# Gathers that take their row numbers straight from the picks, without small index tiles from ScalarE

## The chip, the cores and the metric

The kernel runs on one core of a Trainium2 chip. The metric is the device time of one execution in microseconds. The engines are named as a profile names them: PE (TensorE), DVE (VectorE), ACT (ScalarE), POOL (GpSimd, which here issues the indirect loads) and SP (SyncE, which here issues nearly all other loads and stores). PEld is the loading of weights into PE, which runs beside the matmuls.

## The reference, cut to what matters

One layer of an encoder: two gated token mixers, then a retrieval over 128 x 128 single-neuron experts (PEER). Only the last part is touched by the change. For each of 512 tokens and 8 heads, 16 experts are picked by a product of two sets of 128 keys; each picked expert has a row in `u_tab` and a row in `v_tab`, both 16384 x 1024 in float32.

```
q = (t @ w_q).reshape(n_tok, PEER_HEADS, 2, PEER_HALF)
sc = jnp.einsum("thpk,hpnk->thpn", q, sub_keys)
s_top, i_top = lax.top_k(sc, PEER_TOPK)
...
idx = jnp.take_along_axis(cand_idx..., pos, axis=-1)      # 8 heads x 16 picks for each token
g = jax.nn.softmax(best, axis=-1)
ue = u_tab[ib]
act = jax.nn.gelu(jnp.einsum("phkd,pd->phk", ue, tb))
ve = v_tab[ib]
out = jnp.einsum("phk,phkd->pd", gb * act, ve)
```

## The kernel before

The 512 tokens are four tiles of 128. Tiles 1 to 3 (384 tokens) are done **densely**: every one of the 16384 experts is multiplied with every token, and a gate matrix that is zero outside the picks selects. Tile 0 is done by **gathers**: for each of its 128 picks per token (8 heads x 16), an indirect load brings 128 rows of `u_tab` (one for each token of the tile, 512 KB) and later 128 rows of `v_tab` into a row buffer in SBUF, and DVE consumes it. That is 256 gathers, `ru0` to `ru127` and `rv0` to `rv127`.

The program has four parts in time: the mixers (to about 400 us), the keys and picks (to about 580), the gate matrix (to about 798), and the **last stage**, a loop over 128 **key pairs** `i` (one block of 128 rows of `v_tab`). For each `i` of the last stage:

- SP loads `raw_v` (512 KB, seven `raw` buffers shared with `raw_u`), `gt` (the gates, 128 KB, four buffers) and, for the late `i`, `hr` (192 KB); ACT and DVE split `raw_v` into `hi_v` and `lo_v` (three buffers, shared with the split of `raw_u`).
- DVE makes `wf` from gates and activations (L849, L850), ACT rounds it to `wh` (L851), DVE takes the rest `wl` (L852).
- PE does 18 matmuls of 512 columns into six accumulators (`v_mm`, L831, L832, L835).
- For the first 66 of the 128 pairs there is also one block of `u` to be turned into activations (`h_tile`, L392): `raw_u`, `hi_u`, `lo_u`, then 24 matmuls of 384 columns (L147 to L149), then a gelu into `hg`.
- Gathers are stepped: `gather_steps(pace[i], GLEFT)` records `pace[i]` gathers and, for each, the DVE instruction (L373 for `ru`, L387 for `rv`, SCALAR_TENSOR_TENSOR, called **the consumption** below) of the gather that lies four back (`drain(left)` with `GLEFT` = 4).

Eight gathers are made in the gate stage. The other 248 are spread over the pairs by weight, 2 for a pair with an `h_tile` and `GTAIL` = 0.5 after that:

```python
    wts = [2 if i < NKEY - nlag else GTAIL if i < NKEY - 4 else 0 for i in range(NKEY)]
    pace, done = [], 0
    for i in range(NKEY):
        want = -(-ng * sum(wts[:i + 1]) // sum(wts))
        pace.append(int(want) - done)
```

The row buffers of the last stage come from two pools in turn, three in `gp` (`GR`) and four in `dp` (`DR`), so an even gather reuses the buffer of the gather six before it, an odd one that of the gather eight before it. Gathers run in the order of `gsched`: 32 of `u`, 16 of `v`, and then 16 of `u` and 16 of `v` in turn, to the last 16 of `v`.

Up to the last stage the order on each engine is written by hand (`pinned()`). In the last stage it is not: the build places the instructions on each engine by its own reckoning of when their inputs are there. Only instructions that are given to `tc.keep_in_program_order` keep their place among each other: the gathers on POOL, and before the change the index tiles on ACT.

An index tile `eix` is a copy of up to four columns of picks (`eall`, float32) to int32, made by ACT in key pair `i` for the gathers of that pair (`gather_release`, L658 to L670). `ei0` holds the same picks as int32 for all 128 columns; it is finished in the second part of the program.

Of the kernel before, what the change touches and what calls it, by code (L numbers as in the profile page):

```python
# [11 lines left out]
I32 = mybir.dt.int32  # L12
U32 = mybir.dt.uint32
AF = mybir.ActivationFunctionType
# [3 lines left out]
P = 128  # L18
# [42 lines left out]
def tile_block(ctx: ExitStack, tc: tile.TileContext, x, w_in, vecs, w_ax, w_out, n2row, w_q, skT,  # L61
               uT, u_tab, v_tab, frow, out):
    nc = tc.nc
    sync, act, dve, pool, pe = nc.sync, nc.scalar, nc.vector, nc.gpsimd, nc.tensor
# [33 lines left out]
    def load(src, name, nsub=None):  # L98
        raw = strm.tile([P, D], F32, tag="raw", name=f"raw_{name}", bufs=RB)
        dst = raw if nsub is None else raw.rearrange("p (a b) -> p a b", a=nsub)  # L100
        sync.dma_start(dst, src)
        return raw

    def split(raw, name, lo_eng, pl=None):
        hi = (pl or strm).tile([P, D], F32R, tag="hi", name=f"hi_{name}", bufs=SB)
        lo = (pl or strm).tile([P, D], F32R, tag="lo", name=f"lo_{name}", bufs=SB)
        act.activation(hi, raw, AF.Copy)  # L107
        lo_eng.tensor_tensor(lo, raw, hi, op=ALU.subtract)  # L108
        return hi, lo
# [237 lines left out]
    eall = gp.tile([P, NTT, P], F32, name="eall")  # L347
    gall = gp.tile([P, NTT, P], F32, name="gall")
    ei0 = gp.tile([P, P], I32, name="ei0")
# [2 lines left out]

    ha = ctx.enter_context(tc.tile_pool(name="ha", bufs=1))

    gidx = {}
    rpool = [(gp, GR)]
    gcnt = [0]

    def gather(tab, n, name):
        ix = gidx.get(name, ei0[:, n:n + 1])  # L360
        rp, nb = rpool[gcnt[0] % len(rpool)]
        gcnt[0] += 1
        rows = rp.tile([P, D], F32, tag="rows", name=name, bufs=nb)
        ins = pool.indirect_dma_start(out=rows, out_offset=None, in_=tab,  # L364
                                in_offset=bass.IndirectOffsetOnAxis(ap=ix, axis=0))
        tc.keep_in_program_order(ins)
        return rows
# [8 lines left out]
    def drain(left):  # L376
        while len(dq) > left:
            dq.pop(0)()
# [31 lines left out]
    def h_get(i):  # L410
        if i not in hg:
            hg[i] = ha.tile([P, TD], F32, tag="hg", name=f"hr{i}", bufs=AHEAD)
            sync.dma_start(hg[i], hd[i - (NKEY - SPILL)])
        return hg[i]
# [230 lines left out]
    gsched = []  # L645
# [9 lines left out]
        gsched.append((gather_v, n))  # L655
    gpos = [0]

    def gather_release(n, i):  # L658
        names, p = [], gpos[0]
        while len(names) < n and p < len(gsched):  # L660
            f, a = gsched[p]
            if f is not gather_w:
                names.append(("ru" if f is gather_u else "rv") + str(a))
            p += 1
        if names:
            t = dp.tile([P, 4], I32, tag="eix", name=f"eix{i}", bufs=4)
            for m, nm in enumerate(names):
                c = int(nm[2:])
                tc.keep_in_program_order(act.activation(t[:, m:m + 1], eall[:, 0, c:c + 1], AF.Copy))  # L669
                gidx[nm] = t[:, m:m + 1]  # L670

    def gather_steps(n, left=0):
        while n > 0 and gpos[0] < len(gsched):
            f, a = gsched[gpos[0]]
            f(a)
            drain(left)
            gpos[0] += 1
            if f is not gather_w:
                n -= 1
# [108 lines left out]
    dp = ctx.enter_context(tc.tile_pool(name="dp", bufs=1))  # L788
# [7 lines left out]
    pace, done = [], 0  # L796
# [43 lines left out]
    for i in range(NKEY):  # L840
        raw = vr.pop(i) if i in vr else load(v_tab[i * P:(i + 1) * P, :], f"v{i}")
        hi, lo = split(raw, f"v{i}", dve)
        gt = dp.tile([P, TG], F32, tag="gt", name=f"gt{i}", bufs=4)
        sync.dma_start(gt, gd[i])
        wf = dp.tile([P, TD], F32, tag="wf", name=f"wf{i}", bufs=2)
        wh = strm.tile([P, TD], F32R, tag="wh", name=f"wh{i}", bufs=3)
        wl = strm.tile([P, TD], F32R, tag="wl", name=f"wl{i}", bufs=3)
        hv_ = h_get(i)
        dve.tensor_tensor(wf[:, :TG], gt, hv_[:, :TG], op=ALU.mult)  # L849
        dve.tensor_tensor(wf[:, TG:], stg[:, i, :], hv_[:, TG:], op=ALU.mult)  # L850
        act.activation(wh, wf, AF.Copy)  # L851
        dve.tensor_tensor(wl, wf, wh, op=ALU.subtract)  # L852
        if i < NKEY - LATE:
            for t in range(NDT):
                v_mm(i, t, hi, lo, wh, wl)
        else:
            late.append((hi, lo, wh, wl))
        if hn < NKEY:
            h_tile(hord[hn], dve)
            hn += 1  # L860
        gather_release(pace[i], i)
        gather_steps(pace[i], GLEFT)
        if i == NKEY - LATE - 1:
            for j in range(i + 1, NKEY):
                vr[j] = load(v_tab[j * P:(j + 1) * P, :], f"v{j}")
            fgb = dp.tile([P, D], F32, tag="rows", name="fgb", bufs=DR)
            sync.dma_start(fgb, frow.partition_broadcast(P))
            x2s.extend(load(x2d[t], f"x2s{t}") for t in range(NTT))
            x2s.append(dp.tile([P, D], F32, tag="rows", name="junk", bufs=DR))
            drain(0)  # L870
            finish(0)
# [50 lines left out]
```

## Time and profile before

| | us |
|---|---|
| median of 3 runs | 1619.49 (1616.62 to 1621.41) |
| the profiled execution | 1619.77 |
| its span, first to last instruction | 1617.7 |
| PE busy | 1597.2 (99%) |
| DVE busy | 1265.1 (78%) |
| ACT busy | 688.3 (43%) |
| POOL busy | 517.1 (32%) |

The granted clock of PE was 0.999 of full over the span. Matmuls are pipelined, so that a matmul's own duration is about twice the distance to the next one; "busy" therefore hides short gaps, and the distance between key pairs on PE is the better measure.

### The profile page before, as it was taken

Reading aid. Unit: us, or ns where it says so; the run is one execution under the profiler, and the core shown is the slowest. Engines: PE = TensorE matmul, PEld = TensorE weight load, DVE = VectorE, ACT = ScalarE, POOL = GpSimd, SP = SyncE. Lnnn points to the kernel's source line nnn. Section 1 sums busy time; section 2 is a strip of 40 time slices with the busy share of each in tenths; the row PEclk is TensorE's granted clock in tenths of the full one; section 3 lists DMA queues with packets and bytes.
Section 4 is the critical chain, followed back from the end, with each engine's and each line's share of the span. In section 5 each row is a group of like instructions: output and inputs, shape, how many; then the busy total and the mean of one; then the engine's idle time right before and its main releaser. Section 6 shows DMA issues by size and latency. Waiting matters only on the chain.

```text
span 1617.7 us, 23570 instructions
## 1 busy us (share of the span) xinstructions
PE 1597.2 (99%) x8402; PEld 1411.7 (87%) x8402; DVE 1265.1 (78%) x2404; ACT 688.3 (43%) x1222; POOL 517.1 (32%) x379
## 2 busy tenths in 40 slices
PE   9999999999999999999999999999999999999998
PEld 8888888888988999999999889999988998788776
DVE  6666666635999998676878888888888888777776
ACT  7444444434333454444533433333343443333334
POOL 0000000003787840000044444546544554223321
PEclk9999999999999999999999999999999999999999
DMA  6222222334333356969499999999999999998884
GB/s 242 95 94 95 95 95 95 91 112 175 107 124 111 126 177 191 305 214 301 153 324 323 342 328 332 341 332 334 340 323 350 324 347 367 328 308 292 289 304 150
DMA packets 158453, 379.09 MB, mean 234 GB/s; under 512 B 14080, under 2 KB 78592, under 8 KB 158208
## 3 DMA queue, kind: packets, MB, share of 16 engines
q1 hardware_dynamic: 112832, 230.25, 41.5%
q0 software_dynamic: 36864, 134.23, 23.6%
q10 hardware_dynamic: 8640, 13.11, 2.3%
q8 instruction: 65, 1.06, 0.3%
q14 instruction: 52, 0.43, 0.1%
HBM read 345.56 MB, written 31.98 MB: 233 GB/s over the span
## 4 chain that ended last, share of the span: by engine, by line
PE 64%; DMA 12%; DVE 10%; issue 6%; POOL 3%; ACT 2%; SPq 2%; DVEq 0%; ACTq 0%; POOLq 0%
PE pin L149 6%; PE pin L148 6%; PE pin L147 6%; PE ph L147 6%; PE ph L149 6%; PE ph L148 6%; PE acc L832 6%; PE acc L835 5%; PE acc L831 5%; DMA rv<-in_v_tab_dram,eix 5%; DMA ru<-in_u_tab_dram,eix 4%; DMA gd<-stg 2%; PE pq L147 2%; PE pq L149 2%; PE pq L148 2%
## 5 line engine op out<-in xcount | busy, mean ns | idle before, releaser
L147 PE MATMUL ph<-a1h,hi_u 128*128 128x384 f32 x1024 | 346.2, 338 | 0.0
L149 PE MATMUL ph<-a1h,lo_u 128*128 128x384 f32 x1024 | 343.6, 336 | 0.4 <-POOL lo_u L108 0.4
L148 PE MATMUL ph<-a1l,hi_u 128*128 128x384 f32 x1024 | 342.7, 335 | 0.0
L832 PE MATMUL acc<-lo_v,wh 128*128 128x512 f32 x768 | 301.4, 392 | 5.9 <-DVE lo_v L108 5.7
L831 PE MATMUL acc<-hi_v,wh 128*128 128x512 f32 x768 | 299.5, 390 | 0.0
L364 POOL DMA_INDIRECT rv<-in_v_tab_dram,eix x128 | 171.8, 1342 | 258.0 <-ACT eix L669 211.1
L835 PE MATMUL acc<-hi_v,wl 128*128 128x512 f32 x768 | 238.8, 390 | 0.0
L364 POOL DMA_INDIRECT ru<-in_u_tab_dram,eix x120 | 163.8, 1365 | 218.6 <-ACT eix L669 186.1
L387 DVE SCALAR_TENSOR_TENSOR acc<-rv,w,acc 128x1024 f32<-128x1024 f32 x128 | 164.7, 1287 | 81.3 <-DMA rv<-in_v_tab_dram,eix 81.2
L107 ACT ACTIVATE hi_v<-raw_v 128x1024 fp32r<-128x1024 f32 x128 | 135.0, 1054 | 184.2 <-PE ph L148 166.6
L373 DVE SCALAR_TENSOR_TENSOR ru<-ru,t 128x1024 f32<-128x1024 f32 x128 | 155.5, 1222 | 52.7 <-DMA ru<-in_u_tab_dram,eix 50.1
L148 PEld LDWEIGHTS ph<-a1l,hi_u 128*128 128x128 f32 x1024 | 192.4, 188 | 2.6
L147 PEld LDWEIGHTS ph<-a1h,hi_u 128*128 128x128 f32 x1024 | 192.3, 188 | 2.6
L149 PEld LDWEIGHTS ph<-a1h,lo_u 128*128 128x128 f32 x1024 | 192.2, 188 | 1.2 <-POOL lo_u L108 0.8
L851 ACT ACTIVATE wh<-wf 128x384 fp32r<-128x384 f32 x128 | 67.1, 525 | 269.8 <-PE acc L832 181.0
L832 PEld LDWEIGHTS acc<-lo_v,wh 128*128 128x128 f32 x768 | 144.2, 188 | 40.7 <-DVE lo_v L108 12.1
L149 PE MATMUL pin<-a1h,lo_in 128*128 128x512 f32 x448 | 174.4, 389 | 0.3 <-POOL lo_in L108 0.3
L148 PE MATMUL pin<-a1l,hi_in 128*128 128x512 f32 x448 | 174.4, 389 | 0.0
L147 PE MATMUL pin<-a1h,hi_in 128*128 128x512 f32 x448 | 174.3, 389 | 0.0
L835 PEld LDWEIGHTS acc<-hi_v,wl 128*128 128x128 f32 x768 | 144.1, 188 | 30.7
L831 PEld LDWEIGHTS acc<-hi_v,wh 128*128 128x128 f32 x768 | 144.1, 188 | 27.3 <-ACT hi_v L107 0.2
L108 DVE TENSOR_TENSOR lo_v<-raw_v,hi_v 128x1024 fp32r<-128x1024 f32 x128 | 156.1, 1219 | 2.7 <-ACT hi_v L107 2.6
(199 smaller groups left out, 2470.2 us busy)
## 6 DMA issues: line engine op xcount, KB each, us to landing
raw_u<-in_uT_dram SPq DMA_DIRECT2D x128, 512.0 KB
raw_v<-in_v_tab_dram SPq DMA_DIRECT2D x128, 512.0 KB
raw_in<-in_w_in_dram SPq DMA_DIRECT2D x56, 512.0 KB
gd<-stg SPq DMA_DIRECT2D x8, 2048.0 KB
gt<-gd SPq DMA_DIRECT2D x128, 128.0 KB
hd<-hg ACTq DMA_DIRECT2D x56, 192.0 KB
hr<-hd SPq DMA_DIRECT2D x56, 192.0 KB
raw_q<-in_w_q_dram SPq DMA_DIRECT2D x16, 512.0 KB
```

The costliest lines, as they stand in the source:

```text
L107: act.activation(hi, raw, AF.Copy)
L108: lo_eng.tensor_tensor(lo, raw, hi, op=ALU.subtract)
L147: pe.matmul(pt, wh(k), xh(k), start=start and m == 0, stop=False)
L148: pe.matmul(pt, wh(k), xl(k), start=False, stop=False)
L149: pe.matmul(pt, wl(k), xh(k), start=False, stop=stop and m == n - 1)
L364: ins = pool.indirect_dma_start(out=rows, out_offset=None, in_=tab, in_offset=bass.IndirectOffsetOnAxis(ap=ix, axis=0))
L373: dq.append(lambda: dve.scalar_tensor_tensor(rows, rows, 1.0, t0, op0=ALU.mult, op1=ALU.mult, accum_out=d0[:, n:n + 1]))
L387: dq.append(lambda: dve.scalar_tensor_tensor(acc0, rows, w0[:, n:n + 1], acc0, op0=ALU.mult, op1=ALU.add))
L831: pe.matmul(accs[t][h], wh[:, ts], hi[:, hsl], start=first, stop=False)
L832: pe.matmul(accs[t][h], wh[:, ts], lo[:, hsl], start=False, stop=False)
L835: pe.matmul(accs[t][h], wl[:, ts], hi[:, hsl], start=False, stop=last)
L851: act.activation(wh, wf, AF.Copy)
```

## The change

The index tiles are gone, with the ACT instructions that made them; every gather takes its row numbers from `ei0`.

```diff
-    gidx = {}
     rpool = [(gp, GR)]
     gcnt = [0]
 
     def gather(tab, n, name):
-        ix = gidx.get(name, ei0[:, n:n + 1])
+        ix = ei0[:, n:n + 1]
...
-    def gather_release(n, i):
-        names, p = [], gpos[0]
-        while len(names) < n and p < len(gsched):
-            f, a = gsched[p]
-            if f is not gather_w:
-                names.append(("ru" if f is gather_u else "rv") + str(a))
-            p += 1
-        if names:
-            t = dp.tile([P, 4], I32, tag="eix", name=f"eix{i}", bufs=4)
-            for m, nm in enumerate(names):
-                c = int(nm[2:])
-                tc.keep_in_program_order(act.activation(t[:, m:m + 1], eall[:, 0, c:c + 1], AF.Copy))
-                gidx[nm] = t[:, m:m + 1]
...
-        gather_release(pace[i], i)
         gather_steps(pace[i], GLEFT)
```

PE's order is the same before and after. On the other engines the build places instructions differently. In the rows below the number after a tile's first name is its key pair or gather; `lo_v36` is the split of pair 36, `ru64` the 65th gather of `u`.

DVE in the middle of the last stage, before: the seven rows up to the split of key pair 36.

```order
L852 TENSOR_TENSOR wl37_10742<-wf37_10740,wh37_10741 128x384
L849 TENSOR_TENSOR wf39_10904<-gt39_10902,hg39_10480 128x256
L387 SCALAR_TENSOR_TENSOR acc0_7785<-rv46_10486,w0_2927,acc0_7785 128x1024
L108 TENSOR_TENSOR lo_u41_10610<-raw_u41_10607,hi_u41_10609 128x1024
L387 SCALAR_TENSOR_TENSOR acc0_7785<-rv47_10489,w0_2927,acc0_7785 128x1024
L373 SCALAR_TENSOR_TENSOR ru64_10492,d0_2928<-ru64_10492,t0_2535 128x1024
L108 TENSOR_TENSOR lo_v36_10656<-raw_v36_10653,hi_v36_10655 128x1024
```

The same place after the change.

```order
L372 SCALAR_TENSOR_TENSOR ru90_11405,d0_2928<-ru90_11405,t0_2535 128x1024
L837 TENSOR_TENSOR wl37_10591<-wf37_10589,wh37_10590 128x384
L372 SCALAR_TENSOR_TENSOR ru91_11408,d0_2928<-ru91_11408,t0_2535 128x1024
L108 TENSOR_TENSOR lo_u41_10467<-raw_u41_10464,hi_u41_10466 128x1024
L834 TENSOR_TENSOR wf39_10744<-gt39_10742,hg39_10345 128x256
L835 TENSOR_TENSOR wf39_10744<-stg2_7120,hg39_10345 128x128
L372 SCALAR_TENSOR_TENSOR ru92_11477,d0_2928<-ru92_11477,t0_2535 128x1024
L372 SCALAR_TENSOR_TENSOR ru93_11480,d0_2928<-ru93_11480,t0_2535 128x1024
L108 TENSOR_TENSOR lo_v36_10509<-raw_v36_10506,hi_v36_10508 128x1024
```

Ahead of `lo_v36` the last consumption was that of `ru64`, the 113th gather of the order of `gsched`, and is now that of `ru93`, the 158th. The splits and the `wf`, `wl` of the same pairs stand around it as before. Counted over a longer piece: from `lo_v12` to `lo_v54`, 42 key pairs, DVE's order held the consumptions from `rv6` (39th) to `rv72` (169th), 130 of them, and now holds those from `ru39` (56th) to `rv104` (233rd), 177 of them.

DVE where the last gather is consumed, before.

```order
L387 SCALAR_TENSOR_TENSOR acc0_7785<-rv126_15205,w0_2927,acc0_7785 128x1024
L852 TENSOR_TENSOR wl122_15218<-wf122_15216,wh122_15217 128x384
L108 TENSOR_TENSOR lo_v122_15211<-raw_v122_15208,hi_v122_15210 128x1024
L849 TENSOR_TENSOR wf124_15291<-gt124_15289,hr124_15294 128x256
L850 TENSOR_TENSOR wf124_15291<-stg2_7120,hr124_15294 128x128
L387 SCALAR_TENSOR_TENSOR acc0_7785<-rv127_15245,w0_2927,acc0_7785 128x1024
```

And after the change.

```order
L386 SCALAR_TENSOR_TENSOR acc0_7785<-rv124_14738,w0_2927,acc0_7785 128x1024
L108 TENSOR_TENSOR lo_v59_12244<-raw_v59_12241,hi_v59_12243 128x1024
L386 SCALAR_TENSOR_TENSOR acc0_7785<-rv125_14811,w0_2927,acc0_7785 128x1024
L386 SCALAR_TENSOR_TENSOR acc0_7785<-rv126_14849,w0_2927,acc0_7785 128x1024
L837 TENSOR_TENSOR wl61_12403<-wf61_12401,wh61_12402 128x384
L386 SCALAR_TENSOR_TENSOR acc0_7785<-rv127_14887,w0_2927,acc0_7785 128x1024
```

The last consumption stood behind `lo_v122` and now stands between `lo_v59` and `lo_v60`: all 256 gathers are consumed ahead of pair 60, and none is left for the 62 pairs that have no `h_tile`.

DVE at the end of the gate stage, after the change (`oij` and `o12` are the one-hot tiles from which PE makes the last gates).

```order
L372 SCALAR_TENSOR_TENSOR ru5_6875,d0_2928<-ru5_6875,t0_2535 128x1024
L701 TENSOR_TENSOR oij_46_7648<-io_5173,ij_5218 128x2048
L703 TENSOR_TENSOR o12_46_7649<-oij_46_7648,g12_5219 128x2048
L701 TENSOR_TENSOR oij_47_7652<-io_5173,ij_5218 128x2048
L372 SCALAR_TENSOR_TENSOR ru8_7861,d0_2928<-ru8_7861,t0_2535 128x1024
L703 TENSOR_TENSOR o12_47_7653<-oij_47_7652,g12_5219 128x2048
L732 TENSOR_TENSOR lo_u5_7656<-raw_u5_7121,hi_u5_7606 128x1024
```

The consumption of `ru8` stands between the two halves of the last one-hot; before the change it stood behind `lo_v2`, and these two stood side by side.

## Rows read from the trace of the kernel before

**Rows 1.** The first page of the profile: the span, the busy time of four engines with its share of the span, and two lines of 40 equal slices of the span (40.4 us each): the busy tenths of the 16 DMA engines, and the GB/s that they moved.

```profile
span 1617.7 us, 23570 instructions
PE 1597.2 (99%) x8402; PEld 1411.7 (87%) x8402; DVE 1265.1 (78%) x2404; ACT 688.3 (43%) x1222; POOL 517.1 (32%) x379
DMA  6222222334333356969499999999999999998884
GB/s 242 95 94 95 95 95 95 91 112 175 107 124 111 126 177 191 305 214 301 153 324 323 342 328 332 341 332 334 340 323 350 324 347 367 328 308 292 289 304 150
```

**Rows 2.** Stretches of the last stage, cut where PE begins a key pair. Columns: start and end in us, length, busy us and instructions of PE, PEld, DVE, ACT, POOL, then the granted clock, the DMA busy share and GB/s. The first is pairs 0 to 58, the second ten pairs of it (20 to 29), the third pairs 59 to 65, the fourth pairs 66 to 126, the last seventeen pairs of those (79 to 95).

```profile
798.30:1291.68 493.38, 492.03 (x2480) 445.62 (x2480) 413.14 (x577) 192.34 (x421) 236.49 (x179) 1.00 0.93 330
965.77:1048.83 83.06, 83.06 (x421) 75.64 (x421) 71.01 (x96) 32.59 (x71) 40.74 (x31) 1.00 0.96 339
1291.68:1349.80 58.12, 58.12 (x296) 52.96 (x296) 50.24 (x67) 23.00 (x51) 28.75 (x22) 1.00 0.95 340
1349.80:1605.80 256.00, 251.50 (x1099) 205.28 (x1099) 197.28 (x322) 98.37 (x182) 70.32 (x47) 1.00 0.85 296
1400.24:1469.60 69.36, 69.36 (x308) 57.45 (x306) 51.58 (x83) 26.28 (x48) 18.62 (x13) 1.00 0.90 308
```

**Rows 3.** Who waited for whom, over the whole span: engine, tile and line, what it waited for, us in total, times, longest.

```profile
POOL rv L364 <- ACT eix L669: 211.1, 56, 8.4
POOL ru L364 <- ACT eix L669: 186.1, 43, 42.9
DVE acc L387 <- DMA rv<-in_v_tab_dram,eix: 81.2, 54, 4.9
DVE ru L373 <- DMA ru<-in_u_tab_dram,eix: 50.1, 45, 3.2
```

**Rows 4.** Four consecutive pieces of the chain that ended last, around a late key pair: start, us, what.

```profile
1162.88 9.24 DMA rv<-in_v_tab_dram,eix
1172.51 0.90 issue
1173.41 1.23 DVE lo_v L108
1174.69 0.50 PE acc L832
```

**Rows 5.** The index copies on ACT, and the gathers on POOL in the last stage: line, engine, operation, tiles, count, busy us or times, then (second and third row) idle time before them and what ended it.

```profile
L669 ACT ACTIVATE eix<-eall x248: 185/191/203, 808.0 to 1576.8; 128x1 int32<-128x1 f32 x124
L364 POOL DMA_INDIRECT rv<-in_v_tab_dram,eix x128 | 171.8, 1342 | 258.0 <-ACT eix L669 211.1 <-issue 18.0 <-DVE acc L387 11.8
L364 POOL DMA_INDIRECT ru<-in_u_tab_dram,eix x120 | 163.8, 1365 | 218.6 <-ACT eix L669 186.1 <-issue 20.4 <-DVE wl L852 7.2
```

**Rows 6.** DVE in order of time around the end of the gate stage and at the first gather of the last stage: start, us, instruction, and in brackets the idle time before it.

```profile
782.91 1.22 DVE L373 SCALAR_TENSOR_TENSOR ru<-ru,t 128x1024 f32<-128x1024 f32 x1
784.06 0.08 DVE L373 DVE_READ_ACCUMULATOR ru<-ru,t 128x1 f32 x1
...
786.46 1.22 DVE L716 TENSOR_TENSOR oij<-io,ij 128x2048 f16<-128x2048 f16 x1
787.71 1.22 DVE L718 TENSOR_TENSOR o<-oij,g 128x2048 f16<-128x2048 f16 x1
...
789.99 1.22 DVE L373 SCALAR_TENSOR_TENSOR ru<-ru,t 128x1024 f32<-128x1024 f32 x1
791.13 0.08 DVE L373 DVE_READ_ACCUMULATOR ru<-ru,t 128x1 f32 x1
...
813.64 1.23 DVE L373 SCALAR_TENSOR_TENSOR ru<-ru,t 128x1024 f32<-128x1024 f32 x1 [1.54 <-DMA ru<-in_u_tab_dram,eix]
```

**Rows 7.** POOL in order of time: the first gather of the last stage, and the one of rows 4.

```profile
808.92 0.94 POOL L364 DMA_INDIRECT ru<-in_u_tab_dram,eix  x1 [42.89 <-ACT eix L669]
...
1162.88 1.69 POOL L364 DMA_INDIRECT rv<-in_v_tab_dram,eix  x1 [0.30 <-ACT hi_u L107]
```

**Rows 8.** DVE in order of time around the consumption of that gather.

```profile
1172.21 1.28 DVE L387 SCALAR_TENSOR_TENSOR acc<-rv,w,acc 128x1024 f32<-128x1024 f32 x1 [0.71 <-DMA rv<-in_v_tab_dram,eix]
1173.41 1.22 DVE L108 TENSOR_TENSOR lo_v<-raw_v,hi_v 128x1024 fp32r<-128x1024 f32 x1
```

**Rows 9.** The groups of DVE instructions in pairs 20 to 29 (965.77 to 1048.83): count, busy us, mean ns of one, idle time before them and what ended it.

```profile
L387 DVE SCALAR_TENSOR_TENSOR acc<-rv,w,acc 128x1024 f32<-128x1024 f32 x16 | 20.6, 1286 | 7.6 <-DMA rv<-in_v_tab_dram,eix 7.6
L373 DVE SCALAR_TENSOR_TENSOR ru<-ru,t 128x1024 f32<-128x1024 f32 x15 | 18.4, 1226 | 4.4 <-DMA ru<-in_u_tab_dram,eix 4.3
```

**Rows 10.** Stretches around the change from pairs with an `h_tile` to pairs without one; columns as in rows 2, the last two being the DMA busy share and GB/s.

```profile
1358.00:1370.16 12.16, 12.16 (x55) 9.96 (x54) 10.65 (x19) 4.35 (x8) 5.32 (x5) 1.00 1.04 409
1345.00:1380.00 35.00, 33.91 (x156) 28.33 (x154) 31.10 (x49) 12.85 (x26) 15.05 (x12) 1.00 1.01 380
1341.49:1378.46 36.97, 36.97 (x170) 31.14 (x169) 31.74 (x48) 14.56 (x31) 16.74 (x13) 1.00 1.00 376
```

## The prediction

> **What bounds the kernel now.** The first page [rows 1] shows PE busy 99% of the span, and DMA near full from slice 21 on, about 330 GB/s: the last stage uses both. How tight each is, a page over the whole span cannot say, so I cut the last stage where PE begins key pairs [rows 2]. Ten undisturbed pairs with an `h_tile` take 83.06 us, 8.31 each (421 matmuls, 42 a pair), and seventeen without one 69.36 us, 4.08 each (18 matmuls a pair). That is PE's own pace. The stage loses little against it: pairs 0 to 58 take 493.38 us where 59 x 8.306 is 490.1, so 3.3 us are lost; the next seven lose nothing (58.12 against 58.1); pairs 66 to 126 take 256.0 where 61 x 4.08 is 248.9, so 7.1 are lost. **No more than 10.4 us of the stage can be won.**
>
> Who is late when PE loses? The waits [rows 3] show POOL idle 397 us for `eix`, which costs nothing by itself, and DVE idle 131 us for gathers that have not landed. The chain [rows 4] links one to the other: a gather lands, DVE consumes it, then does `lo_v`, and PE's matmul with `lo_v` starts. So the losses come from gathers issued late: that of rows 4 goes out at 1162.88 and is consumed at 1172.21 [rows 7, 8], 9.3 us later, and DVE waited for it.
>
> **The change part by part.** *The copies.* 248 instructions of 0.191 us [rows 5], 47 us, leave ACT, which is 43% busy [rows 1]. No link of the chain above is theirs, so I count 0.
>
> *The wait of POOL for `eix`.* It goes, and POOL next waits for the row buffer. But `eix` did a second thing. The copies were held in program order on ACT, behind the work of their key pair, and so the build could place no gather, and no consumption, ahead of it. The order of DVE after the change shows what follows: from `lo_v12` to `lo_v54` there are 177 consumptions in 42 pairs, 4.21 a pair, where there were 130, 3.10 a pair, and the last stands ahead of `lo_v60`. DVE runs its list in order, so PE cannot have `lo_v` of a pair before those gathers have landed and been consumed. The weights of `pace` no longer spread the gathers over 124 pairs; they are pressed into some 59. I price that from three sides.
>
> *DVE.* Pairs 20 to 29 hold 31 consumptions [rows 9], and DVE is busy 71.01 us in them [rows 2], 7.10 a pair. From one to the next instruction a consumption takes 1.14 us for `ru` (789.99 to 791.13 [rows 6]) and 1.20 for `rv` (1172.21 to 1173.41 [rows 8]), 1.17 in the mean. 1.11 more of them are 1.30 us: 8.40 a pair, just above PE's 8.31.
>
> *DMA.* A pair loaded `raw_v` and `raw_u` of 512 KB, `gt` of 128 and 3.10 gathers of 512: 2739 KB or 2.80 MB, at 8.31 us 338 GB/s, and the row says 339 [rows 2]. With 4.21 gathers it is 3308 KB, 3.387 MB. What can DMA move when pressed? The trace has such a stretch where the pairs without `h_tile` begin and SP runs ahead: 409 GB/s over 12 us, 380 over 35, 376 over 37 [rows 10], at shares from 1.00 to 1.04. That is 8.28, 8.91 and 9.01 us a pair. The other end is the 339 at a share of 0.96 [rows 2], if the share is read as room: 9.99. I take 380, 8.91 us, because it is a long stretch at a full share with loads and gathers mixed, and because DVE, at 8.40 of 8.91, can no longer make up a late landing.
>
> The Trainium skill has a lower figure: DMA: Bandwidth & Descriptors, Where 436 GB/s comes from, lets the memory side bind transfers between HBM and SBUF at about 358 GB/s for a core. By it a pair would take 9.46 us and the sum below would end near 1681. The stretch of 35 us at 380 [rows 10] lies above that figure, so the trace does not bear it out as a ceiling.
>
> *Row buffers and POOL.* Six gathers pass in 6 x 8.91 / 4.21 = 12.7 us, and a buffer's round holds issue to consumption (9.3 us above, under load), the consumption (1.2) and 0.3 for POOL to start: 10.8. POOL needs 4.21 x (1.35 + 0.30) = 6.9 us a pair [rows 5, 7]. Neither decides at this pace.
>
> *The start.* `ru8` is now consumed inside the gate stage, ahead of the last `o12`. Its buffer is that of `ru5`, free at 784.1 [rows 6]; the first gather of the stage took 4.72 us from issue (808.92 [rows 7]) to consumption (813.64 [rows 6]), so `ru8` is there at 788.9 at the earliest, while DVE gets to it at 787.7 [rows 6]. 1.2 us of wait and 1.15 of consumption push the last gates back: +2.3. If PE has work left there it costs 0, and at 9.3 us from issue 6.9; I take 2.3, since that transfer runs beside few others.
>
> *The pairs without gathers.* From pair 60 on DVE has no gather to wait for, and the loads of a pair (`raw_v`, `gt`, `hr`: 832 KB in 4.08 us, 209 GB/s) are far below what rows 10 show. Of the 7.1 us lost there I give back 6.5; the rest I leave to the finish of tile 0, which DVE does ahead of the last splits in both orders.
>
> **The sum**, against the profiled execution's own 1619.77 us (0.3 us above the median of 1619.49): start +2.3; 59.4 pairs at 8.91 in place of 8.31, +35.6; the 3.3 lost there before is within the new pace, -3.3; pairs 66 on, -6.5. Together +28.1, which gives **1648 us**.
>
> **The rivals.** *DMA keeps up.* Then DVE sets the pace, 8.40: +2.3 + 59.4 x 0.09 - 9.8 = -2.2, 1618 us, no change. It decides if DMA moves 3.387 MB in 8.40 us, 403 GB/s, for 500 us on end. For it: 409 over 12 us. Against it: 376 to 380 as soon as the stretch is three times as long, and that gathers depend on DVE, which would have no idle time left. The Trainium skill would speak for it: Perfetto Trace Analysis, Roofline, says that a core that is active alone may go past its share of the memory, up to some 435 GB/s. By that a pair's loads would take 7.8 us and this rival would come true; the best row here is 409.
>
> *The waits go and nothing takes their place* (the other side). DVE's idle 131 us are what gathers cost; take them away, and PE keeps 8.31 and 4.08 throughout: -9.8, 1610 us. It decides if DVE gets through a pair with 4.21 consumptions in 8.31 us and DMA moves 408 GB/s. My DVE figure misses that by only 0.09, but both would have to be better than their rows.
>
> *DMA gives what it gave.* At 339 GB/s a pair takes 9.99 us: +2.3 + 59.4 x 1.68 - 9.8 = +92, 1712 us. For it speaks the share of 0.96; against it the same rows 10. Between 339 and 370 lies all that DVE and DMA lose by waiting for each other.
>
> *Row buffers bind.* If issue to consumption grows past 11.2 us (12.7 less 1.5), the round of six sets the pace. At 13 us six gathers take 14.5, a pair 10.2: +2.3 + 59.4 x 1.87 - 9.8 = +104, 1723 us. The longest lead in the rows is 9.3, under three gathers at once; six would be longer.
>
> **How the numbers follow.** The forecast, 370 to 393 GB/s or 8.62 to 9.15 us a pair, gives 1630 to 1662 and gets 0.60. DMA at 339 to 370: 0.19, 1662 to 1712. Row buffers: 0.05. DVE alone, 1618, with little either way: 0.11. Faster: 0.05. A measurement of this kernel can tell about 0.3%, or 5 us, from no change. So slower 0.84, same 0.11, faster 0.05. The range of 8 in 10 leaves out the faster case and half of the flat one below, and the row buffers and the slowest of the DMA case above: 1620 to 1700.
>
> **What would show it.** Right: PE's pairs 1 to 59 stand some 8.9 us apart, evenly late, DMA at a share of 1.00 and 370 to 390 GB/s there; POOL waits for DVE (row buffers); the last gather goes out near 1320 us in place of 1577; from pair 60 on pairs take 8.31 and then 4.08 without a gap, DMA near 210 GB/s. Wrong in the order: gathers still run beyond pair 66. Wrong in the price of DMA: over 400 GB/s for hundreds of us, pairs at 8.4 and DVE without idle time. Wrong in the buffers: DMA below full while POOL waits for DVE and DVE for landings.

## The result and the profile after

The changed kernel takes 1638.08 us (median of 5 runs, 1636.63 to 1638.35); before, it took 1620.44 (5 runs, 1616.62 to 1624.55). The ratio is **1.0102, 95% interval 1.0082 to 1.0121**: slower by about 1%, 17.6 us. The forecast was 1648 with a range of 1620 to 1700. So the side is right and the size is 10 us off, and the trace shows that most of the loss came in another way than the prediction's.

The page after, the lines that answer to [rows 1] (the slices are 40.9 us each):

```profile
span 1635.7 us, 23146 instructions
PE 1600.6 (98%) x8402; PEld 1416.7 (87%) x8402; DVE 1263.4 (77%) x2404; ACT 666.6 (41%) x974; POOL 520.1 (32%) x379
DMA  6222222334332357877699999999999965667662
GB/s 240 94 93 94 94 94 94 97 110 180 110 115 103 127 191 222 278 246 259 250 406 384 398 378 400 393 356 406 355 387 371 406 216 183 210 210 210 209 201 102
```

ACT has 248 instructions fewer. DMA moves 355 to 406 GB/s in twelve slices, where it moved some 330 before, and then some 210. That is the pressing together that was forecast: the gathers end twelve slices into the stage (the last goes out at 1307.7 us, near the 1320 that was forecast). But the prediction held 380 GB/s to be all that DMA gives over long stretches, and here whole slices stand at 400 to 406, with others between them at 355 to 371.

Stretches of the last stage, columns as in [rows 2]: pairs 0 to 15, 16 to 30, 31 to 33 (with the latest one), 34 to 39, 47 and 48 (with the second latest); then all of pairs 0 to 59, the six pairs 60 to 65, and pairs 66 to 126.

```profile
803.01:936.00 132.99, 132.99 (x674) 120.97 (x673) 127.43 (x190) 48.24 (x68) 86.15 (x65) 1.00 1.01 396
936.00:1066.59 130.59, 126.07 (x632) 113.03 (x632) 125.10 (x174) 44.51 (x62) 89.10 (x64) 1.00 1.01 391
1066.59:1099.24 32.65, 27.30 (x128) 24.76 (x127) 27.45 (x38) 8.85 (x12) 18.80 (x15) 0.90 0.95 347
1099.24:1149.08 49.84, 49.84 (x254) 45.38 (x253) 44.79 (x61) 17.86 (x25) 35.05 (x25) 1.00 1.02 402
...
1211.16:1233.16 22.00, 18.32 (x86) 16.54 (x85) 17.35 (x25) 5.90 (x8) 11.92 (x9) 0.92 0.93 338
...
803.01:1324.79 521.78, 505.07 (x2521) 456.56 (x2521) 493.29 (x682) 178.52 (x249) 329.84 (x242) 0.99 1.00 384
1324.79:1374.63 49.84, 49.84 (x253) 45.38 (x253) 21.27 (x30) 17.70 (x24) 0.00 (x0) 1.00 0.45 149
1374.63:1623.81 249.18, 249.18 (x1099) 205.93 (x1099) 143.22 (x252) 96.17 (x134) 0.00 (x0) 1.00 0.64 197
```

Three things are to be seen. The first sixteen pairs take 132.99 us, 8.31 each: the undisturbed pace of [rows 2] with 4.2 gathers to a pair in place of 3.1. The mean over pairs 0 to 59 is 8.70 (521.78 / 60), but hardly any pair runs at 8.7: 50 of the 60 are within 0.3 us of 8.31, and the loss sits in ten late ones, where PE stands still (27.30 of 32.65 us busy, 18.32 of 22.00). And behind pair 59 POOL has nothing left (x0) and PE loses nothing.

Span against span: the stage starts at 803.01 in place of 798.30 (+4.7), pairs 0 to 65 take 571.6 in place of 551.5 (+20.1), and pairs 66 to 126 take 249.2 in place of 256.0 (-6.8). The sum is 18.0, the whole difference of the spans (1635.7 and 1617.7).

Now one late pair. The chain there (start, us, what):

```profile
1070.76 1.21 DVE acc L386
1071.97 0.26 issue
1072.22 8.53 DMA ru<-in_u_tab_dram,ei
```

DVE in order of time at the same place, and then POOL. In brackets: idle time ahead of the instruction, and what ended it.

```profile
1070.68 2.60 DVE L386 SCALAR_TENSOR_TENSOR acc<-rv,w,acc 128x1024 f32<-128x1024 f32 x2
1073.19 1.22 DVE L108 TENSOR_TENSOR lo_v<-raw_v,hi_v 128x1024 fp32r<-128x1024 f32 x1
1074.33 1.32 DVE L386 SCALAR_TENSOR_TENSOR acc<-rv,w,acc 128x1024 f32<-128x1024 f32 x1
1080.78 1.23 DVE L372 SCALAR_TENSOR_TENSOR ru<-ru,t 128x1024 f32<-128x1024 f32 x1 [5.13 <-DMA ru<-in_u_tab_dram,ei]
1081.93 0.08 DVE L372 DVE_READ_ACCUMULATOR ru<-ru,t 128x1 f32 x1
1081.93 0.55 DVE L837 TENSOR_TENSOR wl<-wf,wh 128x384 fp32r<-128x384 f32 x1
1082.40 1.28 DVE L386 SCALAR_TENSOR_TENSOR acc<-rv,w,acc 128x1024 f32<-128x1024 f32 x1
```

```profile
1069.73 1.30 POOL L363 DMA_INDIRECT rv<-in_v_tab_dram,ei  x1 [0.30 <-issue]
1072.22 1.86 POOL L363 DMA_INDIRECT ru<-in_u_tab_dram,ei  x1 [1.19 <-DVE acc L386]
```

And the first matmul on PE that needed what DVE does after that (`lo_u`, the split behind the last row of DVE above):

```profile
1084.87 0.69 PE L149 MATMUL ph<-a1h,lo_u 128*128 128x384 f32 x1 [5.34 <-DVE lo_u L108]
```

Read the first consumption at 1070.68: it frees a row buffer at about 1071.9, and POOL, which has waited for it, issues a gather into it at 1072.22. Only two more consumptions stand in DVE's order between that one and the gather's own. DVE is ready at 1075.65 and waits 5.13 us for a gather that has been under way for 3.4. The consumption behind it, at 1082.40, is of an `rv` that was gathered **ahead** of this `ru`: the `ru` is consumed out of turn. DVE's wait reaches PE, which stands still for 5.34 us.

The order of DVE's instructions after the change has 30 of the 256 consumptions out of the order of their gathers; before there are none. They stand at seven places: `ru8` ahead of the last `o12` of the gate stage (and of `ru6` and `ru7`), and `ru32`, `ru48`, `ru64`, `ru80`, `ru96`, `ru112`, each the first of a run of `u` gathers, moved two or three places ahead of `v` gathers that go out before it. Before, the copies were pinned on ACT (`keep_in_program_order` ties an instruction behind the one recorded just ahead of it on its engine), and the gathers behind them. After, the build is free to order the consumptions itself.

This gives **theory A1**: the loss is that of consumptions out of turn, whose row buffer comes free too late. Its rival, **A2**, is the prediction's: 4.2 gathers to a pair are more than DMA or DVE can carry.

### The profile page after: what moved, and what is told of

Read it like the earlier page. It is cut to its first block, busy times and chain, and to the rows that moved or that the text cites. A ratio compares the mean times of both kernels' runs of the same rounds, so it can differ in the third digit from the quotient of the medians.

```text
span 1635.7 us, 23146 instructions
## 1 busy us (share of the span) xinstructions
PE 1600.6 (98%) x8402; PEld 1416.7 (87%) x8402; DVE 1263.4 (77%) x2404; ACT 666.6 (41%) x974; POOL 520.1 (32%) x379
## 4 chain that ended last, share of the span: by engine, by line
PE 62%; DVE 13%; DMA 11%; issue 7%; POOL 5%; SPq 1%; ACT 1%; DVEq 0%; ACTq 0%; POOLq 0%
PE acc L817 7%; PE acc L820 7%; PE acc L816 7%; PE pin L149 6%; PE pin L147 6%; PE pin L148 6%; PE ph L149 4%; PE ph L147 4%; PE ph L148 4%; DMA rv<-in_v_tab_dram,ei 4%; POOL ru L363 4%; DMA ru<-in_u_tab_dram,ei 3%; DVE ru L372 2%; DMA raw_v<-in_v_tab_dram 2%; PE pq L147 2%
## 5 line engine op out<-in xcount | busy, mean ns | idle before, releaser
L363 POOL DMA_INDIRECT ru<-in_u_tab_dram,ei x128 | 183.4, 1433 | 291.3 <-DVE ru L372 241.1
L363 POOL DMA_INDIRECT rv<-in_v_tab_dram,ei x128 | 168.3, 1315 | 85.1 <-DVE acc L386 47.5
L820 PEld LDWEIGHTS acc<-hi_v,wl 128*128 128x128 f32 x768 | 144.1, 188 | 30.6
```

Source lines behind the costliest of these rows:

```text
L820: pe.matmul(accs[t][h], wl[:, ts], hi[:, hsl], start=False, stop=last)
```

## The experiments

Late pairs are told below as what PE's distance from one key pair to the next exceeds 8.31 us by (first `acc` matmul to first `acc` matmul in the trace).

**1. Copies made, but not read.** The kernel before, with one line of the change: the gathers read the picks. ACT still makes all 248 copies.

```
-        ix = gidx.get(name, ei0[:, n:n + 1])
+        ix = ei0[:, n:n + 1]
```

> The kernel before, with its 248 index copies on ACT kept, but no gather reads them: every gather reads ei0. The build then gives DVE the same order as after the change (4.21 consumptions a key pair, the last ahead of pair 60). Theory A (what costs is the order that the build makes once the copies no longer hold the gathers; the 47 us of ACT are worth nothing): within 3 us of the kernel after, 1635 to 1641, some 18 us slower than before. Rival (the copies' own time on ACT, or the wait of POOL for them, is what sets the time before): another time than the kernel after, by more than 4 us.

1632.91 us (before in the same job: 1619.63, 13 runs), ratio 1.0067 [1.0045, 1.0089]. ACT is busy 687.5 us with 1222 instructions, as before, and most of the loss is there all the same: 13.3 us above before, where the changed kernel is 17.6 above (by the medians). That is 2 us below the expected stretch and 5 below the changed kernel, so by its letter the rival's sign ("by more than 4 us") came true. But the copies that are kept make the kernel faster than the changed one, which is not how a cost of ACT would show. DVE has the same order of tensor instructions as after, 30 consumptions out of turn; the 5 us lie in other losses at the same places (table below), smaller in sum, and why they differ was not found. So ACT's time is not what makes the loss; that the gathers no longer depend on the copies is.

**2. One copy in each key pair.** The kernel before, but only the first gather of a pair has and reads a copy (110 copies; the other 138 gathers read the picks).

```
-            for m, nm in enumerate(names):
+            for m, nm in enumerate(names[:1]):
```

> The kernel before, but only the first gather of a key pair reads an index copy made by ACT in that pair; the others read ei0 (POOL is in order, so they stand behind it). DVE's order is that of the kernel before. Theory A: the time of the kernel before, within 4 us (1616 to 1624), with fewer than half of the copies. Rival (the copies cost ACT time that is on the path): faster than before by over 5 us.

1620.58 us, ratio 0.9998 [0.9985, 1.0012]: as before. No consumption out of turn, and the gathers spread over all pairs as before. One pinned copy in a pair does for the order what all of them do.

**3. All consumptions in turn.** The changed kernel, and each consumption tied behind the one recorded ahead of it. The tie sets the order on DVE alone; it adds no wait on the chip.

```
+    used = []
+
+    def in_turn(ins):
+        if used:
+            tc.add_manual_dep(ins.ins, used[-1].name, ...NoSync...)
+        used.append(ins.ins)
...
-        dq.append(lambda: dve.scalar_tensor_tensor(acc0, rows, ...))
+        dq.append(lambda: in_turn(dve.scalar_tensor_tensor(acc0, rows, ...)))
```

> The kernel after, with one thing added: DVE's consumptions keep the order of the gathers among each other (no wait, an order alone). In the kernel after 30 of 256 stand out of turn, at the end of the gate stage and at the six places where a run of v gathers is followed by u gathers; there a u gather is consumed two or three places early. The rate stays: 4.2 a key pair, all by pair 61. Theory A1 (the pairs that PE loses in the kernel after, 23 us in lumps at pairs 17 to 53, and the 4.7 us at the start, come from the consumptions out of turn, since a u gather then has 3 to 4 us instead of 10 between its buffer coming free and its consumption): key pairs at 8.31 to 8.4 nearly throughout, 1609 to 1617. Theory A2, that of the prediction (4.2 gathers a pair are more than DMA or DVE can carry beside the rest): lumps or a slower pace stay, 1628 or more.

**1612.19 us** (1611.22 to 1612.78), ratio 0.9939 [0.9919, 0.996]: 26 us below the changed kernel and 7 below before. The gathers are still pressed together: 255 of 256 consumptions stand ahead of `lo_v60`. The stretches of pairs 0 to 65, of pairs 66 to 126, and from 850 to 1280 us:

```profile
798.45:1349.44 550.99, 549.41 (x2774) 498.89 (x2773) 516.51 (x714) 196.15 (x273) 348.00 (x243) 1.00 0.97 378
1349.44:1598.65 249.21, 249.21 (x1100) 205.93 (x1100) 143.47 (x252) 96.36 (x134) 0.00 (x0) 1.00 0.64 197
...
850.00:1280.00 430.00, 428.43 (x2161) 388.62 (x2160) 423.88 (x574) 152.29 (x212) 310.69 (x214) 1.00 1.02 402
```

In the last of them DMA moves 402 GB/s for 430 us at a share of 1.02, DVE is busy 423.88 of 430.00, and PE loses 1.6 us. A2 falls: at that rate the gathers pass, if they come in turn. DVE's waits for landings tell the same, over the last stage up to 1330 us, first of the changed kernel and then of this one:

```profile
DVE ru L372 <- DMA ru<-in_u_tab_dram,ei: 24.6, 11, 5.1
DVE acc L386 <- DMA rv<-in_v_tab_dram,ei: 2.2, 4, 0.9
```

```profile
DVE ru L379 <- DMA ru<-in_u_tab_dram,ei: 4.4, 7, 1.1
DVE acc L393 <- DMA rv<-in_v_tab_dram,ei: 1.5, 4, 0.6
```

**4. In turn, and spread.** Number 3, and from the ninth consumption on each is also pinned behind the DVE instruction recorded ahead of it, so that the weights of `pace` hold again (3.1 consumptions to a pair).

```
+        if len(used) >= 8:
+            tc.keep_in_program_order(ins)
```

> The kernel after, with consumptions in turn and each also kept behind what is recorded ahead of it on DVE, so that their rate is again that of pace (3.1 a key pair with an h_tile, 0.77 after that), without index copies: gathers are held by row buffers alone. Theory A1 and A2: gathers go out earlier than before the change, DVE no longer waits for them, PE runs 8.31 and 4.08 us a pair without a gap: 10 us below the kernel before, 1608 to 1613. Rival (gathers that go out early take DMA from the loads of raw_v, gt and hr): no faster than before, 1618 or more, with DVE or ACT waiting for those loads.

**1611.12 us** (1610.06 to 1611.24), ratio 0.9935 [0.9915, 0.9954].

```profile
797.45:1345.69 548.24, 548.24 (x2774) 499.20 (x2773) 471.68 (x651) 196.48 (x271) 275.23 (x204) 1.00 0.94 338
1345.69:1595.16 249.47, 249.47 (x1100) 205.92 (x1100) 193.01 (x310) 95.98 (x134) 51.66 (x41) 1.00 0.82 288
```

PE is busy in every microsecond of both stretches, with DMA at a share of 0.94. The microsecond between it and number 3 is too little for these runs to tell apart; both beat before and after.

**5. One place undone: `ru8`.** The changed kernel with the tie of number 3 for the first ten consumptions only.

```
+        if used and len(used) < 10:
```

> The changed kernel with one of its seven places undone: a tie holds the first ten consumptions on VectorE in the order of their gathers, so ru8 no longer stands ahead of the last one-hot tile. The six other places (u32, u48, u64, u80, u96, u112 ahead of pending v gathers) stay as they are. Theory A (each place costs what its gather is short of in lead): the first key pair starts at about 798.3 again instead of 803.0, the lumps of the key pairs stay at some 20 us, 1638.1 - 4.7 = 1633.4. Rival (the start only moves loss about, the later lumps grow by what the start gives back, since the gathers are paced by row buffers anyway): 1637 to 1639.

1628.86 us (before in this job: 1624.11, 10 runs), ratio 1.0038 [1.0021, 1.0055]; A1 had said 1633.4. The stage starts at 798.22, so the 4.7 us of the start are `ru8`'s. The other 4.6 us are won among the later pairs (567.0 us for pairs 0 to 65 in place of 571.6), which I had not expected, and they lead to the rule of the next part: with one consumption moved, the build moves the other places too. 25 consumptions are out of turn, `ru80` now only one place, and pair 33, 7.7 us late in the changed kernel, is no longer late.

**6. One place alone.** Number 3, with `ru112` and `ru113` left out of the tie; 5 consumptions are out of turn.

```
+        if len(used) in range(208,210):
+            used.append(used[-1])
+            return
```

> The kernel of e3 (all consumptions in turn, 1612.2) with one place freed again: u112 and u113 are left out of the tie, and u112 then stands ahead of v93 to v95, three consumptions behind the one that frees its row buffer, as it does in the changed kernel; 5 of 256 consumptions are out of turn. Theory A: one lump near key pair 48, of 5.4 us as in the changed kernel, and no other over 1 us: 1612.2 + 5.4 = 1617.6. Rival (the places work on each other: the queue of gathers falls behind at the earlier ones, and a single one is caught by the lead that has been kept): under 1 us, 1612 to 1613.

1616.44 us, ratio 0.9953 [0.9935, 0.997]; against before, number 3 stood at 0.9939, a difference of 2.3 us where 5.4 were expected (before was 1624.11 in this job and 1619.63 in that one). The profile says why: one late pair, 49, by 5.92 us, and no other, while number 3 loses 2.7 us in small pieces at pairs 38 to 53 that are gone here. The stretch of the gather, and the one ahead of it:

```profile
1189.52:1211.00 21.48, 18.50 (x81) 16.03 (x80) 17.19 (x24) 5.32 (x8) 12.31 (x9) 0.84 0.92 337
850.00:1190.00 340.00, 340.00 (x1721) 309.66 (x1720) 336.21 (x459) 121.52 (x169) 242.45 (x171) 1.00 1.03 404
```

and DVE there:

```profile
1192.63 1.28 DVE L396 SCALAR_TENSOR_TENSOR acc<-rv,w,acc 128x1024 f32<-128x1024 f32 x1
1198.16 1.23 DVE L382 SCALAR_TENSOR_TENSOR ru<-ru,t 128x1024 f32<-128x1024 f32 x1 [4.26 <-DMA ru<-in_u_tab_dram,ei]
```

340 us without a gap, then DVE waits 4.26 us for the one gather out of turn. It needs no other late place ahead of it.

**What the price of a place hangs on.** For each consumption I counted, in DVE's order, how many consumptions it stands behind the one that frees its row buffer (three buffers of one pool and four of another, taken by turns; POOL issues in order, so a gather also waits for those ahead of it). In turn that is 6 or 7 through the last stage, before and in numbers 3 and 4 (but for the first five of the stage, `ru8` to `ru12`, at 3 to 5 in every kernel that has them in turn). At the places, with pieces under 0.8 us away from them left out:

```
place (about pair)      ru32 (10)  ru48 (18)  ru64 (26)  ru80 (33)  ru96 (41)  ru112 (48)
after: behind               4          4          4          3          3          3
after: late, us             0         3.2        2.2        7.7        3.2        5.4
number 1: behind            4          4          4          3          3          3
number 1: late, us          0         0.7        1.4        7.5        1.0        7.3
number 5: behind            4          3          3          5          4          4
number 5: late, us          0         3.6        6.7         0         2.5        5.3
number 6: behind          in turn    in turn    in turn    in turn    in turn      3
number 6: late, us          0          0          0          0          0         5.9
```

The mean of the nine places that stand 3 behind is 5.4 us, of the nine that stand 4 behind 1.7 (from 0 to 5.3); the one at 5 costs nothing. A consumption comes every 1.98 us (8.31 / 4.2), so 3 are 5.9 us, less the 1.2 of the consumption that frees: 4.7 us for issue and landing, where the gathers of the two latest pairs of the changed kernel took 8.53 us (above) and 8.05 (in the chain at the end of this text). Those are not long landings: the median of number 3 is 8.9 us from 900 to 1280 us. What is short is the lead.

A part of the price is PE's clock. At the places behind which PE waited longest, 5.34 and 3.68 us in the changed kernel and 2.98 in number 6, the pairs are 7.7, 5.4 and 5.9 us late; the rest, 2.4, 1.7 and 2.9 us, goes for the most part with matmuls at the lower level of the clock (the end of this text has one such place). Behind waits of 2.42, 1.90 and 1.43 us in the changed kernel the granted clock stayed at 1.00, and the rest is about 0.3 us.

**7 and 8. More bytes, first try.** Number 3 with one load more in each of the first 60 pairs, of 128 KB and of 256 KB. To make room, `gt` has three buffers in the one and two in the other, in place of four.

```
+        if i < 60:
+            ex = dp.tile([P, 256], F32, tag="ex", name=f"ex{i}", bufs=1)
+            sync.dma_start(ex, u_tab[i * P:(i + 1) * P, :256])
```

> The kernel of e3 with one more load of 128 KB into a tile that nobody reads, in each of the first 60 key pairs (the tile gt has three buffers instead of four to make room). A pair then moves 3.52 MB instead of 3.39. Theory A (the DMA engines stood at their limit of some 409 GB/s, and e3 just fits): 3.52 MB / 409 GB/s = 8.60 us a pair instead of 8.31, 60 x 0.29 = 17 us, 1629. Theory B (they have room left; 405 GB/s is only what the pairs asked for): 1612 to 1614, and 420 GB/s in the pairs. Theory C (380 GB/s was the right price and e3 escaped by its order): 3.52 MB / 380 = 9.26, 57 us, 1669.

> As e7 with 256 KB more in each of the first 60 key pairs (gt has two buffers): 3.65 MB a pair. Theory A: 3.65 MB / 409 GB/s = 8.92 us a pair, 60 x 0.61 = 37 us, 1649, and the step from e7 to e8 is as large as or larger than that from e3 to e7. Theory B: 1612 to 1616, and 435 GB/s in the pairs. Theory C: 3.65 MB / 380 = 9.6, 77 us, 1689.

1696.97 us (1.0456 [1.0434, 1.0477]) and 1701.91 (1.0466 [1.0433, 1.0498]): none of the three theories. The SyncE queue's own waits of number 7, from 800 to 1320 us:

```profile
SPq L840 <- DMA ex<-in_u_tab_dram: 199.2, 54, 6.2
```

The build had drawn the loads, which nobody reads, into the first 25 pairs, where each held up SyncE's queue until the load ahead of it had landed. DMA moved some 300 GB/s there. It measures a queue that is blocked, not a rate, and so tells nothing of A2; it is the same trap as in the changed kernel, an instruction that nothing ties to its place.

**9 and 10. More bytes, spread.** The same, each load pinned behind the `gt` of its pair; `gt` has three and two buffers as in numbers 7 and 8.

```
-            sync.dma_start(ex, u_tab[i * P:(i + 1) * P, :256])
+            tc.keep_in_program_order(sync.dma_start(ex, u_tab[i * P:(i + 1) * P, :256]))
```

> e7 again with each of the 60 added loads of 128 KB tied behind the load of gt of its own key pair: in e7 the build had drawn them together into the first 25 pairs, where SyncE's queue stood waiting for one to land before it issued the next, so e7 told nothing of the rate. Same edit otherwise. Theory A (e3 stands at the limit of the DMA engines, about 409 GB/s): 3.52 MB a pair / 409 GB/s = 8.60 us instead of 8.31, 60 x 0.29 = 17 us above e3, 1629, and 405 to 410 GB/s in the pairs. Theory B (room left): 1612 to 1614, and 420 GB/s. Theory C (380 GB/s is the price): 9.26 us, 1669.

> e8 again with the added loads of 256 KB spread in the same way, one to a pair. Theory A: 3.65 MB a pair / 409 GB/s = 8.92 us, 60 x 0.61 = 37 us above e3, 1649, twice the step of e9. Theory B: 1612 to 1616. Theory C: 9.6 us, 1689.

1638.42 us (1.0098 [1.0075, 1.0121]) and 1654.22 (1.02 [1.0178, 1.0222]), before in this job 1621.26. Above number 3, by the ratios to before, 26 and 42 us; 17 and 37 were expected of a limit at 409 GB/s. Number 9 and then 10, from 900 to 1280 us:

```profile
900.00:1280.00 380.00, 362.51 (x1802) 322.14 (x1801) 359.05 (x494) 125.55 (x177) 238.14 (x181) 1.00 1.03 400
```

```profile
900.00:1280.00 380.00, 356.34 (x1752) 312.10 (x1751) 349.58 (x484) 122.16 (x172) 231.62 (x175) 1.00 1.03 404
```

With more bytes asked for, DMA still moves 400 to 404 GB/s at a share of 1.03, and the pairs become longer. So the limit in this mix is at about 404 GB/s: less than my 409, more than the prediction's 380. The 3.38 MB that a pair asks for with 4.2 gathers come to 8.37 us at 404, PE's 8.31 almost to the point (from 850 to 1280 us number 3 has 4.13 gathers to a pair, 3.34 MB); the changed kernel stands on the edge of what DMA carries, and 128 KB more are over it. Two other causes were built in with the bytes, and the traces speak against both. SyncE's queue waits for the added loads (155 us in number 9, 99 in number 10), but in all it waits no longer than without them (435 and 442 us from 800 to 1320 us, 459 in number 3). And DVE, from 900 to 1280 us, waits for landings of gathers alone (19.5 and 30.6 us, 4.8 in number 3), never for `gt` with its fewer buffers. ACT waited 16 us for `raw_v` in number 9, so that of its 26 us not all need be the gathers' landing; in number 10 it is 3 us.

**11. Fewer row buffers, in turn.** Number 3 with two buffers in the second pool in place of four.

```
-DR = 4
+DR = 2
```

> e3 (all consumptions in turn) with five row buffers instead of seven in the last stage: each gather's buffer is then freed four or five consumptions ahead of the gather's own turn, instead of six or seven; order and pace of the instructions stay the same. Theory A (what counts is how many consumptions lie between the freeing and the turn, not that they are out of turn): 4 to 5 x 1.98 us = 7.9 to 9.9 us, less 2.4 us for the consumption that frees and the issue, leaves 5.5 to 7.5 us for a landing that took 8 us in the lumps of the changed kernel, so nearly every second gather is late: with landings of 8 us, (8 + 2.4) / 4.5 = 2.3 us for each consumption instead of 1.98, 9.7 us a pair, +80 us, 1690; with landings of 6.5 us since fewer are under way, 1.98, and the loss is small, 1612 to 1620. Taken: 1640. Rival (in turn, two row buffers fewer cost nothing): 1612 to 1613.

1689.62 us, ratio 1.0418 [1.0382, 1.0453]. DVE's order is that of number 3, no consumption is out of turn, and each stands 4 or 5 behind the one that frees its buffer.

```profile
900.00:1280.00 380.00, 341.01 (x1635) 295.52 (x1635) 327.31 (x450) 115.06 (x161) 217.91 (x164) 0.99 0.96 347
```

DMA is no longer at its limit, and PE loses 39 of 380 us. It came out at the figure for landings of 8 us, not at the 1640 that I took, and that it met the figure so closely is partly luck: the landings there have a median of 7.3 us, and (7.3 + 2.4) / 4.5 would be 2.16 us for a consumption, 9.1 a pair, some 45 us in place of the 77 that it lost. The side is plain all the same: the landings are shorter than number 3's 8.9, and yet DVE waits 69 us for them from 800 to 1320 us, where number 3 waits 6. So it is not being out of turn by itself that costs: what counts is how far the freeing of the buffer lies ahead of the gather's turn, and with 4 or 5 consumptions to the landing all through the stage the loss is there too, in small pieces at nearly every pair.

## Why the prediction was right about the side and wrong about the way

- **What bounds the kernel, and the copies at 0:** right. Number 2 has 138 copies fewer and the same time; number 1 keeps all of them and loses most of what the change loses.
- **The wait for `eix` held the gathers to their pairs; without it they are pressed into 59 pairs:** right. POOL issues nothing after pair 59 (x0), and DMA stands at 149 and then 197 GB/s from there.
- **The pairs, +35.6 and -3.3: the term that failed.** It measured +20.1 (pairs 0 to 65), and it is another thing. The step was "I take 380, 8.91 us, because it is a long stretch at a full share". The mean share of 1.01 hid two parts. The first 10 us of the stretch of [rows 10] have a lower share and a lower rate; the other 25 already move 401 GB/s (columns as in [rows 2], the kernel before):

```profile
1345.00:1355.00 10.00, 10.00 (x51) 8.98 (x50) 8.80 (x11) 4.08 (x12) 4.98 (x4) 1.00 0.95 329
1355.00:1380.00 25.00, 23.91 (x106) 19.34 (x105) 22.30 (x39) 8.77 (x16) 10.07 (x8) 1.00 1.03 401
```

DMA carries 402 to 404 GB/s (numbers 3 and 10), the rival "DMA keeps up" put its point of decision at 403, and pairs 0 to 15 ran at 8.31. That 1638 lies inside the range is luck as far as the mechanism goes: the price that gave 1648 is not to be found in the runs.
- **The 358 and the 435 GB/s that the prediction cites:** the Trainium skill, DMA: Bandwidth & Descriptors, Where 436 GB/s comes from, has 358 GB/s as what binds a core's transfers between HBM and SBUF. The runs show 402 to 404 over 340 to 430 us, so that it was no ceiling here. The Trainium skill, Perfetto Trace Analysis, Roofline, is borne out in that a core active alone goes past its share; its 435 was not reached.
- **DVE at 8.40 a pair:** 1 to 2% too high. Number 3 has it at 423.88 of 430.00 us, 8.19 a pair with 4.13 consumptions; with 4.21 that would be 8.28 (an estimate, at 1.17 us each), which just fits into 8.31.
- **Row buffers, "Six gathers pass in ... 12.7 us":** the second step that failed, and the one behind the loss. Six is right for consumptions in turn. I had the order of DVE after the change and saw in it only `ru8` out of its place; at six more places the turn is broken, three or four consumptions pass, and the buffer's lead is too short for a landing of 8 us (4.7 us at three, above). The rival "row buffers bind" named the right resource but let it fail by a longer landing, everywhere; it failed by a shorter lead, at single places. The prediction's own sign for the buffers ("DMA below full while POOL waits for DVE and DVE for landings") is what the late pairs show, at 347 and 338 GB/s.
- **The start, +2.3:** right in kind, 4.7 in size. `ru8` lands 1.71 us after DVE is ready (1.2 forecast), and its consumption takes 1.15. With 0.3 us by which DVE is later here already, the last gates on PE start 3.1 us later than before (788.99 and 792.11 in the rows below). The other 1.6 us are PE's clock, which the prediction did not have: PE had waited 3.49 us in place of 0.67, and matmuls of 384 columns then come every 0.32 us up to 796.0, in place of 0.17. Number 5 takes back the 4.7. DVE and PE after the change, and the same matmul on PE before:

```profile
789.68 1.23 DVE L372 SCALAR_TENSOR_TENSOR ru<-ru,t 128x1024 f32<-128x1024 f32 x1 [1.71 <-DMA ru<-in_u_tab_dram,ei]
790.83 0.08 DVE L372 DVE_READ_ACCUMULATOR ru<-ru,t 128x1 f32 x1
790.83 1.22 DVE L703 TENSOR_TENSOR o<-oij,g 128x2048 f16<-128x2048 f16 x1
...
792.11 0.23 PE L713 MATMUL pg<-o,oij 128*128 128x128 f16 x1 [3.49 <-DVE o L703]
...
794.15 0.52 PE L149 MATMUL ph<-a1h,lo_u 128*128 128x384 f32 x1
```

```profile
788.99 0.23 PE L728 MATMUL pg<-o,oij 128*128 128x128 f16 x1 [0.67 <-DVE o L718]
```

- **The pairs without gathers, -6.5:** right, -6.8.
- **The rival on the other side,** "the waits go and nothing takes their place", 1610 us: it asked for 8.31 a pair with 4.2 consumptions and 408 GB/s. Number 3 gives 1612 with that very pressing together. Without the copies and with the gathers in turn the kernel gains 7 us; the order that came with the change turns that into a loss of 18.

What stays open: why the build moves just those `u` consumptions ahead (its reckoning was not looked into), and why places with the same count cost from 1.0 to 7.7 us. PE's clock is a part of it, and the rest is not known: number 5's `ru112` at 4 costs as much as the changed kernel's at 3, and number 1 has the changed kernel's order on DVE and loses other amounts at the same places. Gathers just behind a place stand at 4 or 5 as well (`ru116` in number 6 at 4) and are not late there. Whether a place would cost as much with the gathers spread was not run.

## What to carry to other kernels

A small copy that only hands on an index can be what ties a gather to its place; ask of each dependence that is removed what order it held, and tie the order by itself where it is needed (numbers 3 and 4). In a ring of buffers that are filled by gathers, count for each fill how many uses lie between the one that frees its buffer and its own, and compare that time with the landing under load; a use moved three of six places ahead halves it. A mean rate of transfers over a stretch is a floor for what DMA carries, not its limit; its limit shows only where more is asked for.

## What the runs showed of the hardware

DMA moved 404 GB/s for 340 us (number 6) and 402 for 430 us (number 3), gathers and loads mixed, with one core active; asked for 8% more bytes (number 10) it moved 404.

After the waits of 5.34, 3.68, 3.49 and 2.98 us told above PE came back slower. At `ru112` in the changed kernel PE waits 3.68 us for `lo_u`, and then (the chain; start, us, what):

```profile
1208.96 8.05 DMA ru<-in_u_tab_dram,ei
...
1218.26 1.15 DVE lo_u L108
...
1219.46 0.69 PE ph L149
1220.15 0.32 PE ph L147
1220.47 0.32 PE ph L148
...
1222.92 0.18 PE ph L147
1223.10 0.18 PE ph L148
```

Matmuls of 384 columns come every 0.32 us, which is the lower level of the clock (384 columns at 1.2 GHz), up to 1222.5, and then every 0.17 to 0.18, the upper level of 2.4 GHz; the granted clock of the stretch from 1211.16 to 1233.16 is 0.92. About ten matmuls at 0.15 us more each are 1.5 us, so of that pair's 5.4 us some 3.7 are the wait and 1.5 the clock.
